# Making one more operand of the first convolution pair inside the preceding program

## The chip, the cores and the metric

The kernel runs on one NeuronCore of a Trainium2 chip. The metric is the device time of one launch in microseconds (us), as the median of several runs.

## The reference

One hybrid encoder block on a sequence of 1024 tokens with 1024 channels, all in float32. A hidden state h is made from x by an RMS norm and a modulation, and is multiplied by one wide weight matrix. Its columns feed two mixers:

```python
proj = h @ w_in
(a_bg, a_cg, a_x, a_z, q, k, v, z_b, a_raw, b_raw, gate_a_raw, gate_b_raw) = split(proj)

ya = a_cg * dwconv_centred(a_bg * a_x, conv_a_w)      # 3 taps
ya = (ya * silu(a_z)) @ w_pa

o  = gated_delta(q, k, v, g, beta), forwards + backwards   # 8 heads, chunks
yb = (rmsnorm(o) * silu(z_b)) @ w_pb

merged = sigmoid(gate_a_raw) * ya + sigmoid(gate_b_raw) * yb
y = rmsnorm(x + gate * (merged @ w_o))
```

The changed lines belong to a_bg, the first of the four products of the convolution mixer.

## The kernel before

**The stages.** After the loads and the first products comes the heads' program, up to about 758 us: eight heads of the delta rule, with the products for k, q, v, z and for the gates ga0 to ga7, gb0 and gb1 filling TensorE in between. Then follow the convolutions (bg, ax, cg, az for pairs of 128-channel blocks, 16 pairs), two pairs of gates (gb2/gb3 and gb4/gb5), two single gates (gb6, gb7), four pairs of the product with w_pa (called pa), then the products with w_pb and w_o.

**Numbers in two parts.** Each float32 operand is split into `hi`, a rounded copy made by ScalarE (ACT), and `lo`, the rest, a subtraction on VectorE (DVE) or GpSimd (POOL). A product is three matmuls: hi by hi, hi by lo, lo by hi.

**Seven products for a pair.** From the convolutions on, a pair of output blocks by two halves of the tokens is computed as a 2 by 2 block product with seven products instead of eight, named A11, A12, A22, S1, S2, S3 and S4 after their weight operand. The weight operands are sums: S1 = A21 + A22, S2 = S1 - A11, S3 = A11 - A21, S4 = A12 - S2. Each product is 4 x 3 matmuls into a bank of PSUM, and products of one bank accumulate on what is there: S3 follows S2 in its bank after S2's value has been copied out (`u2`), A22 follows S3 after `u3` has been read. The token operands (T1 to T4 and parts of h) are made near the end of the heads' program by `early_sums` (L785); for pa they are loaded again (`yop_B`, `yop_T`) and split on ACT and DVE.

**The first pair.** `early_pair` (L825) loads the raw weights of the first bg pair into free buffers of the heads' program, turns them in place into the sums and makes hi and lo of S4 and S2, and, after the mark "begun", of S1 and A22. The products A11 and A12 run at the end of the heads' program. S3 alone is made behind it, by `pairs[0].prep("S3")` and `rest("S3")` (L1491, L1492) from four loads of its own.

**Order.** In the heads' program the instructions of DVE, ACT, POOL and SP (the queue of most DMAs) are ordered by the kernel's own planner, by priority among what is ready: `early_pair` has priority 3, `early_sums` 4, a smaller number goes first. From the convolutions on, these engines run in the order in which the program is written. In the loop over `steps` (product by product), `advance` makes the weights of the product five steps ahead: `prep` the sums and hi, `rest` lo.

**Buffers.** `xpads` (L459) are three padded rows, used in turn in the heads' program and, two of them, by the convolutions; their four outer columns are zero. The weights of the seven products get their buffers from `slots` (L1288), by a counter that runs through six places and is carried on from pair to pair, into pa:

```python
    place, spare = [4], []
    def slots(name):
        i, place[0] = place[0], (place[0] + 1) % 6
        if i > 3:
            return [btile(p, f"w{p}{name}", 2, dtype=F32R) for p in "hl"]
        if i % 2 == 0 or not spare:
            spare[:] = [wp.tile([P, KT * P], F32R, tag=f"w{p}", name=f"w{p}{name}") for p in ("hi", "lo")]
        return [t[:, ch(i % 2, 512)] for t in spare]
```

The tags `whi` and `wlo` have two buffers each. The same tags serve `wtile` (L1254), which makes whole weights for the single gates gb6 and gb7 four steps before the end of the loop (L1567), and for the products with w_pb. A tile's buffer is free for the next tile of its tag when every instruction of the program that reads or writes the tile, wherever it is written, has run.

**The tail of the loop.** After the last steps (A22, A11, A12, S4 of the pair gb4) the program has, in this order: the splits of the `yop_B` tiles (8), gate 6 (`gate_block(6)`, L1577), four more splits of `yop_B` and four of `yop_T`, the weights of pa's first five products (A11, A12, S4, S2, S1, L1582), gate 7 (L1584), twelve loads of `yop_T`, and the loop over pa's products, which splits two of these tiles a step (T1, then T3, then T4).

Of the kernel before, what the change touches and what calls it, by code (L numbers as in the profile page):

```python
# [9 lines left out]
F32 = mybir.dt.float32  # L10
F32R = mybir.dt.float32r
AF = mybir.ActivationFunctionType
ALU = mybir.AluOpType
# [3 lines left out]
P = 128  # L17
T = 1024
# [310 lines left out]
def block(ctx: ExitStack, tc: tile.TileContext, x, c, wada, wadag, badaT, nwT, win, wab, cva, cvq,  # L329
          alog, dtb, gnw, wpa, wpb, wo, fnw, out, dbg=None):  # L330
    nc = tc.nc
    sched = Scheduler(nc.tensor)
    V, S, G, Q = (Engine(sched, n, e) for n, e in (("dve", nc.vector), ("act", nc.scalar), ("pool", nc.gpsimd),
                                                   ("dma", nc.sync)))
# [33 lines left out]
    def ch(c, w=P):  # L368
        return slice(w * c, w * c + w)
# [13 lines left out]
    def tile_of(pl, shape, tag, name, bufs, dtype=F32):  # L383
        return "tile", pl, shape, tag, name, bufs, dtype
# [11 lines left out]
    weights, wanted, early = {}, [], {}  # L396
# [38 lines left out]
    gc_ = ctx.enter_context(tc.tile_pool(name="gc", bufs=1))  # L435
# [20 lines left out]
    G.affine_select(out=maskB, in_=maskB, pattern=[[-1, P]], compare_op=ALU.is_ge, fill=NEG,  # L456
                    base=0, channel_multiplier=1)
    masks = (maskF, maskB)
    xpads = [gc_.tile([P, T + 4], F32, name=f"xpad{i}") for i in range(2)]  # L459
    for xp in xpads:  # L460
        G.memset(xp[:, 0:2], 0.0)
        G.memset(xp[:, T + 2 : T + 4], 0.0)
# [8 lines left out]
    def rows_of(name, h):  # L471
        return tile_of(gq, [P, T], f"{name}T", f"{name}T{h}", {"k": 3, "q": 2}[name])
# [279 lines left out]
    def big(tag, name, bufs=1, dtype=F32):  # L752
        return tile_of(gp if bufs < 3 else tp, [P, T], tag, name, bufs, dtype)
# [71 lines left out]
    def early_pair():  # L825

        yield "need", ("out", H - 2)
        yield "need", ("pq", H - 1)
        yield "need", ("z", H - 1)
        yield "need", ("w", "bg0")  # L830
        raw = []
        for b, (tag, src) in enumerate((("qT", win[A_BG + 1]), ("tmp", win[A_BG]))):
            t = yield (rows_of("q", H) if tag == "qT" else big(tag, f"first{b}", 2))
            Q.dma_start(t, src)
            raw += [t[:, 0:512], t[:, 512:T]]
        a21, a22, a11, a12 = raw
        V.tensor_tensor(a21, a21, a22, ALU.add)
        V.tensor_tensor(a11, a21, a11, ALU.subtract)
        V.tensor_tensor(a12, a12, a11, ALU.subtract)
        for mark, names, raws in (("filled", ("S4", "S2"), (a12, a11)), ("begun", ("S1", "A22"), (a21, a22))):  # L840
            yield "need", mark
            hi = yield tile_of(wp, [P, KT * P], "whi", f"wh_{names[0]}", 2, F32R)
            lo = yield tile_of(wp, [P, KT * P], "wlo", f"wl_{names[0]}", 2, F32R)
            for i, (n, t) in enumerate(zip(names, raws)):
                h, l = early[n] = [w[:, ch(i, 512)] for w in (hi, lo)]
                S.activation(h, t, AF.Copy)
                V.tensor_tensor(l, t, h.bitcast(F32), ALU.subtract)

    npad = [2]

# [340 lines left out]
    def fill():  # L1191
# [41 lines left out]
        for half, n in enumerate(("A11", "A12")):  # L1233
            ps = early[n] = yield get(pp, f"ps_first_{n}", weights["bg0"][0])
            for m in range(4):
# [3 lines left out]

    sched.run([(chain(h), 0) for h in range(H)] + [(merge(h), 0) for h in range(H)] + [head_out(h) for h in range(H)]  # L1240
              + [g for h in range(H) for g in ((prep_k(h), 1), prep_q(h))] + [fill(), loader(2), (early_pair(), 3), (early_sums(), 4)])
    gctx.close()
    V, S, G, Q, PE = nc.vector, nc.scalar, nc.gpsimd, nc.sync, nc.tensor
# [34 lines left out]
    def btile(tag, name, bufs, shape=(P, 512), dtype=F32):  # L1278
        return late_pools[tag].tile(list(shape), dtype, tag=tag, name=name, bufs=bufs)
# [120 lines left out]
    def mixed(name, j0, place):  # L1400
        seen = [0, 0]

        def full(n, b):
            if (n, b) not in outs:
                outs[n, b] = btile("out", f"{n}{j0 + b}", 4, (P, T))
            return outs[n, b]

        def consume(b, half, ps, add):
            sl = ch(half, 512)
            x = xpads[b][:, 2 + 512 * half : 514 + 512 * half]  # L1410
            seen[b] += 1
            if name in ("bg", "cg"):
                dst = x if name == "bg" else full("c", b)[:, sl]
                if add is None:
                    S.activation(dst, ps, AF.Copy)
                else:
                    V.tensor_tensor(dst, ps, add, ALU.add)
                return
            t = ps
            if add is not None or name == "az":  # L1420
                t = btile("tmp", f"t_{name}{j0}{b}{half}", 2)
                if add is not None:
                    V.tensor_tensor(t, ps, add, ALU.add)
                    ps = t
                if name == "az":
                    S.activation(t, ps, AF.Silu)
            if name == "ax":
                V.tensor_tensor(x, t, x, ALU.mult)
                if seen[b] == 2:
                    acc = full("a", b)  # L1430
                    late.extend(partial(conv3, acc, b, j0 + b, i) for i in range(3))
                return
            c, a = outs["c", b], outs["a", b]
            V.tensor_tensor(t, t, c[:, sl], ALU.mult)
            V.tensor_tensor(a[:, sl], t, a[:, sl], ALU.mult)
            if seen[b] == 2:
                Q.dma_start(y_d[j0 + b], a)
            if sum(seen) == 4:
                rows = [outs.pop((n, b)) for n in ("a", "c") for b in range(2)]
                late.extend([None] * (4 if j0 < 6 else 0) + [partial(y_sum, j0 // 2, i, *rows) for i in range(4)])  # L1440

        return Pair(name, j0, consume, place)

    def y_sum(m, i, a0, a1, c0, c1):
# [31 lines left out]
    pairs = [(n, j) for j in range(0, 8, 2) for n in ("bg", "ax", "cg", "az")]  # L1476
    pairs = [mixed(n, j, None if i else "first") for i, (n, j) in enumerate(pairs)]
# [9 lines left out]
            S.activation(xp[:, 2 + 512 * half : 514 + 512 * half], ps, AF.Sigmoid)  # L1487
        Q.dma_start(sgb_d[j], xp[:, 2 : T + 2])

    pairs[0].ops.update({n: early[n] for n in ("S4", "S2", "S1", "A22")})  # L1490
    pairs[0].prep("S3")  # L1491
    pairs[0].rest("S3")  # L1492
    for n in ("A11", "A12"):
        steps.pop(0)
        pairs[0].after(n, early[n])
# [282 lines left out]
def build(nc, arrays, dbg=None, **kw):  # L1778
    aps = {n: nc.dram_tensor(f"in_{n}", a.shape, mybir.dt.from_np(a.dtype), kind="ExternalInput").ap()
           for n, a in arrays.items()}  # L1780
    out = nc.dram_tensor("out_0_dram", (1, 1024, 1024), F32, kind="ExternalOutput").ap()
    with tile.TileContext(nc, **kw) as tc:
        block(tc, *aps.values(), out, **({"dbg": dbg} if dbg else {}))
# [11 lines left out]
```

## Time and profile before

| what | value |
| --- | --- |
| time, median of 3 runs | 1402.9 us (1399.78 to 1403.99) |
| time of the profiled execution | 1401.2 us |
| its span, first to last instruction | 1399.5 us |
| mean granted TensorE clock | 0.994 |
| PE busy from 778 to 1000 us | 222.00 of 222.00 us |
| PE busy from 1000 to 1160 us | 155.66 of 160.00 us |

The span is what the profile's positions count from; the execution's own time is 1.7 us more. PE is TensorE; matmuls overlap in the pipeline, so a busy PE is not a PE at its peak, but a pause of PE is time lost wherever PE sets the end.

### The profile page before, as it was taken

The numbers are of one execution on the slowest core, as the hardware profiler recorded it, in microseconds if no ns is written. First come the engines' busy times: TensorE is split into PE (matmuls) and PEld (weight loads), VectorE is DVE, ScalarE is ACT, GpSimd is POOL, SyncE is SP. The second block draws the span as 40 slices with busy tenths as digits, with TensorE's granted clock in tenths as the row PEclk, the third lists the DMA queues.
The fourth block names the chain that finished last, engine by engine and source line by source line (L and its number), as shares of the span: only waits on it lengthen the run. The fifth ranks groups of instructions, "written<-read, shape, count | busy, mean of one in ns | idle before, by whom it ended". The sixth has DMA issues, their size and how long they took to land.

```text
span 1399.5 us, 22490 instructions
## 1 busy us (share of the span) xinstructions
PE 1357.9 (97%) x8450; PEld 1132.6 (81%) x8450; DVE 918.7 (66%) x1591; ACT 633.0 (45%) x1543; POOL 461.9 (33%) x702
## 2 busy tenths in 40 slices
PE   5899999999999999999999999999999999999998
PEld 5678888897888888888888788888887878778886
DVE  6868175666758675858585777777787487663335
ACT  5447675564747475654535232232323453323211
POOL 2004847573647565665511000000000100276401
PEclk9999999999999999999999999999999999999999
DMA  9325332505033231414123113131311585595502
GB/s 358 100 56 159 113 80 80 152 32 151 31 88 95 81 102 42 133 41 104 50 103 135 61 54 112 46 120 61 118 49 76 196 300 181 189 333 177 188 15 106
DMA packets 129489, 163.33 MB, mean 117 GB/s; under 512 B 75234, under 2 KB 75618, under 8 KB 129379
## 3 DMA queue, kind: packets, MB, share of 16 engines
q1 hardware_dynamic: 128946, 160.58, 35.5%
q8 instruction: 66, 1.08, 0.3%
q10 hardware_dynamic: 432, 1.31, 0.3%
q14 instruction: 45, 0.36, 0.1%
HBM read 128.16 MB, written 33.69 MB: 116 GB/s over the span
## 4 chain that ended last, share of the span: by engine, by line
PE 88%; DVE 5%; DMA 2%; issue 2%; ACT 1%; POOL 1%; SPq 1%; POOLq 0%; DVEq 0%; ACTq 0%
PE pp_ga L215 6%; PE pp_z L215 6%; PE cb L215 6%; PE pp_q L215 5%; PE pp_v L215 5%; PE pp_k L215 5%; PE ps_cg_S L1353 4%; PE o L215 4%; PE ps_ax_S L1353 4%; PE ps_az_S L1353 4%; PE ps_bg_S L1353 3%; PE ps_pa_S L1353 3%; PE fo L1699 2%; PE fo L1700 2%; PE fo L1701 2%
## 5 line engine op out<-in xcount | busy, mean ns | idle before, releaser
L323 POOL TENSOR_TENSOR E<-E,et 128x30 f32<-128x30 f32 (+7 forms) x240 | 117.5, 490 | 16.9
L1260 POOL TENSOR_TENSOR wl_gb<-wr_gb,wh_gb 128x512 fp32r<-128x512 f32 x4 | 5.6, 1411 | 348.5 <-ACT wh_gb L1259 345.6
L323 POOL TENSOR_TENSOR et<-E 128x30 f32<-128x30 f32 (+7 forms) x240 | 110.2, 459 | 30.8 <-DMA E<-s 14.1
L323 DVE SCALAR_TENSOR_TENSOR S<-S,exps,cb 128x128 f32<-128x128 f32 x96 | 29.7, 344 | 59.7 <-PE cb L215 59.0
L323 ACT ACTIVATE vw<-cb,cols 128x128 f32<-128x128 f32 x112 | 36.1, 363 | 68.8 <-PE cb L215 68.5
L1260 POOL TENSOR_TENSOR wl_pb<-wr_pb,wh_pb 128x512 fp32r<-128x512 f32 x16 | 23.5, 1471 | 119.8 <-ACT wh_pb L1259 119.7
L215 PE MATMUL pp_z<-hhi,wh_z 128*128 128x512 f32 x128 | 52.8, 412 | 0.0
L215 PE MATMUL pp_z<-hhi,wl_z 128*128 128x512 f32 x128 | 52.7, 412 | 0.0
L215 PE MATMUL pp_z<-hlo,wh_z 128*128 128x512 f32 x128 | 52.7, 412 | 0.0
L1270 PE MATMUL pp_pb<-bhi,wl_pb 128*128 128x512 f32 x128 | 50.9, 398 | 1.7 <-POOL wl_pb L1260 1.7
L1269 PE MATMUL pp_pb<-blo,wh_pb 128*128 128x512 f32 x128 | 50.6, 395 | 1.8 <-DVE blo L1550 1.8
L215 PE MATMUL pp_ga<-hhi,wl_ga 128*128 128x512 f32 x128 | 51.7, 404 | 0.0
L215 PE MATMUL pp_ga<-hhi,wh_ga 128*128 128x512 f32 x128 | 51.6, 403 | 0.0
L215 PE MATMUL pp_ga<-hlo,wh_ga 128*128 128x512 f32 x128 | 51.5, 402 | 0.0
L323 DVE SCALAR_TENSOR_TENSOR r<-cb,negeg,vp 128x128 f32<-128x128 f32 x112 | 34.3, 344 | 25.8 <-PE cb L215 25.5
L1268 PE MATMUL pp_pb<-bhi,wh_pb 128*128 128x512 f32 x128 | 51.1, 399 | 0.0
L323 ACT ACT_TABLE_LOAD x38 | 48.8, 1283 | 1.4 <-PEq L1790 0.8
L323 DVE SCALAR_TENSOR_TENSOR vT<-xpad,cvq_t,vT 128x1024 f32<-128x1024 f32 x32 | 48.7, 1522 | 0.3
L215 PE MATMUL pp_q<-hhi,wl_q 128*128 128x512 f32 x112 | 44.9, 401 | 2.2 <-issue 2.2
L323 ACT ACTIVATE vn<-cb,cols 128x128 f32<-128x128 f32 x128 | 41.3, 371 | 10.4 <-PE cb L215 10.4
L323 DVE SCALAR_TENSOR_TENSOR qT<-xpad,cvq_t,qT 128x1024 f32<-128x1024 f32 x32 | 45.7, 1427 | 0.3
L215 PE MATMUL pp_q<-hhi,wh_q 128*128 128x512 f32 x112 | 45.8, 409 | 0.0
(951 smaller groups left out, 4419.7 us busy)
## 6 DMA issues: line engine op xcount, KB each, us to landing
wada<-in_wada SPq DMA_DIRECT2D x16, 512.0 KB, 8.4
D<-gr_d SPq DMA_DIRECT2D x16, 512.0 KB, 6.7
wr_bg<-in_win SPq DMA_DIRECT2D x18, 256.0 KB, 2.7
xt<-in_x SPq DMA_DIRECT2D x8, 512.0 KB, 8.5
wr_k<-in_win SPq DMA_DIRECT2D x16, 256.0 KB, 2.6
wr_q<-in_win SPq DMA_DIRECT2D x16, 256.0 KB, 2.6
wr_v<-in_win SPq DMA_DIRECT2D x16, 256.0 KB, 3.1
wr_ga<-in_win SPq DMA_DIRECT2D x16, 256.0 KB, 2.7
```

What stands on the lines that cost most here:

```text
L215: getattr(self.pe, what)(out, *ins, **kw)
L323: self._sched.record(self._name, lambda: real(*args, **kw), outs, ins, cost, extra, table, op == "memset", port)
L1260: G.tensor_tensor(lo[:, ch(q, 512)], raw, hi[:, ch(q, 512)].bitcast(F32), ALU.subtract)
L1268: PE.matmul(ps, wh, mhi[k][:, sl], start=i == 0, stop=False)
L1269: PE.matmul(ps, wh, mlo[k][:, sl], start=False, stop=False)
L1270: PE.matmul(ps, wl, mhi[k][:, sl], start=False, stop=i == KT - 1)
L1353: PE.matmul(ps, w, r, start=first and m == i == 0, stop=m == 3 and i == 2, skip_group_check=True)
L1699: PE.matmul(ps, mhi[k][:, ch(t)], wh, start=k == 0, stop=False)
L1700: PE.matmul(ps, mlo[k][:, ch(t)], wh, start=False, stop=False)
L1701: PE.matmul(ps, mhi[k][:, ch(t)], wl, start=False, stop=k == KT - 1)
```

## The change

S3 of the first pair joins the four operands that `early_pair` makes. After "begun", and after S1 and A22, it subtracts A11's place (which holds S2) from A22, which gives S3, into the place of A12, and splits it into the two halves of `xpad1`. The loads, the sum and the split behind the heads' program go away, and with them one call of `slots`. `xpad1` becomes a tile that is given up and taken again: the first `consume` that writes to it takes it anew and sets its outer columns to zero.

```diff
-    xpads = [gc_.tile([P, T + 4], F32, name=f"xpad{i}") for i in range(2)]
+    xpads = [sched.place(gc_.tile([P, T + 4], F32, tag=f"xpad{i}", name=f"xpad{i}", bufs=1), gc_, f"xpad{i}", 1) for i in range(2)]
@@ early_pair
                 S.activation(h, t, AF.Copy)
                 V.tensor_tensor(l, t, h.bitcast(F32), ALU.subtract)
+        t = yield tile_of(gc_, [P, T + 4], "xpad1", "first_S3", 1, F32R)
+        h, l = early["S3"] = [t[:, ch(i, 512)] for i in range(2)]
+        V.tensor_tensor(a12, a22, a11, ALU.subtract)
+        S.activation(h, a12, AF.Copy)
+        V.tensor_tensor(l, a12, h.bitcast(F32), ALU.subtract)
+        xpads[1] = None
@@ mixed, consume
             sl = ch(half, 512)
+            if not xpads[b]:
+                xpads[b] = gc_.tile([P, T + 4], F32, tag=f"xpad{b}", name=f"xpad{b}_again", bufs=1)
+                for i in (0, T + 2):
+                    G.memset(xpads[b][:, i : i + 2], 0.0)
@@ behind the heads' program
-    pairs[0].ops.update({n: early[n] for n in ("S4", "S2", "S1", "A22")})
-    pairs[0].prep("S3")
-    pairs[0].rest("S3")
+    pairs[0].ops.update({n: early[n] for n in ("S4", "S2", "S1", "S3", "A22")})
```

## The prediction

> **What bounds the kernel now.** I read the busy totals and the chain of work that ended last first, then the stretch in which the changed weights are used, then who waited for whom on PE.
>
> ```profile
> PE 1357.9 (97%) x8450; PEld 1132.6 (81%) x8450; DVE 918.7 (66%) x1591; ACT 633.0 (45%) x1543; POOL 461.9 (33%) x702
> ...
> PE 88%; DVE 5%; DMA 2%; issue 2%; ACT 1%; POOL 1%; SPq 1%; POOLq 0%; DVEq 0%; ACTq 0%
> ```
>
> TensorE is busy for 97% and is 88% of the chain. An edit on another engine counts only where PE stands still for it, or where it makes PE stand still. So I look for PE's pauses around the edit.
>
> ```profile
> 758.00:778.00 20.00, 17.90 (x76) 13.50 (x77) 16.35 (x26) 8.16 (x15) 0.00 (x0) 1.00 0.53 185
> ```
> ```profile
> PE ps_bg_S L1353 <- ACT u_bg L1359: 1.0, 1, 1.0
> PE ps_ax_S L1353 <- ACT whS_ax L1331: 0.7, 1, 0.7
> PE ps_bg_S L1353 <- DVE u_bg L1361: 0.4, 1, 0.4
> ```
>
> The first row is 758 to 778 us by engine (PE, PEld, DVE, ACT, POOL): PE lacks 20.00 - 17.90 = 2.1 us, and the three waits are those 2.1 us. That is all the change can win at its own place, 0.15% of the run. DVE is the busiest engine behind PE there (16.35 of 20), POOL does nothing.
>
> **Part one: S3 made early.** Removed: four loads, one DVE subtraction, one ACT copy, one DVE rest. Added in the heads' program: again one subtraction, one copy, one rest, and later two small POOL memsets.
>
> ```profile
> 714.67 0.33 SPq L323 DMA_DIRECT2D sga_d<-xpad  x1
> ...
> 754.24 2.25 SPq L1324 DMA_DIRECT2D wr_bg<-in_win  x4
> ```
> ```profile
> 761.10 0.69 DVE L323 TENSOR_TENSOR sums_ktok<-kT,sums_ktok 128x512 fp32r<-128x512 f32 x1
> ...
> 764.29 1.29 DVE L323 TENSOR_TENSOR sums_ktok<-kT,sums_ktok 128x512 fp32r<-128x512 f32 x2
> 765.50 0.69 DVE L1315 TENSOR_TENSOR S_bg<-wr_bg,wr_bg 128x512 f32<-128x512 f32 x1
> 766.89 0.69 DVE L1338 TENSOR_TENSOR wlS_bg<-S_bg,whS_bg 128x512 fp32r<-128x512 f32 x1 [0.70 <-ACT whS_bg L1331]
> 767.50 0.68 DVE L1417 TENSOR_TENSOR xpad<-ps_first_A,e_bg 128x512 f32<-128x512 f32 x1
> ```
> ```profile
> 767.24 0.59 ACT L1359 ACTIVATE u_bg<-ps_bg_S 128x512 f32<-128x512 f32 x1
> ```
> ```profile
> 763.30 0.62 PE L1353 MATMUL ps_bg_S<-sums_ktok,wh_S 128*128 128x512 f32 x2
> ```
>
> The loads cost nothing: S_bg follows the last sums without a bracket, so it waited for its turn on DVE, not for data. What S3 costs today is 767.50 - 765.50 = 2.0 us of DVE: two operations at 0.6 and the 0.70 in which DVE waits for ACT between them. Moved, the operations come ahead of the late sums (priority 3 against 4) and take 2 x 0.6 = 1.2 us there, with no gap because other sums fill it. Gain 2.0 - 1.2 = **0.8 us** for xpad, for u_bg on ACT and so for PE's start on S3; the two later pauses move along. What they push back is covered: sums_ktok, the last one that product S2 needs, ends at 761.8 today and is wanted from 763.30 by PE, 1.5 us of slack for 1.2. Should that cover fail, it costs up to 1.2 us; should the two find idle DVE time, the gain reaches 2.1. The memsets wait for product S3 on an idle POOL, and their columns are read only by the first convolution: nothing. The added wait, for xpad1 to be free, is over by then: of the 32 uses of the three buffers in turn the third-last falls to xpad1, the last ga gate, whose store left SP at 714.67, 40 us earlier. On SP the later loads move up by four, to no use.
>
> **Part two: the shifted places.** The call that goes away also moved a counter. `slots` is called 18 x 7 - 2 - 4 = 120 times in the convolutions and gates before (A11, A12 and the four early operands never call it), 119 times after; call c, from 0, gets place (4 + c) mod 6. Places 4 and 5 have buffers of their own (names wh, wl); 0 and 1, and 2 and 3, are the halves of one tile `whi`/`wlo`, which has two buffers. In between this costs nothing: between 778 and 1000 no wait on PE is listed, and pairs already occur with all six places. At the end it matters. Before, the last call gets place 3, the tile is full. After, the last (S4 of gate pair 4) gets place 2, and the **next call, A11 of the first pa pair, gets place 3: the second half of that same old tile**, though both `wtile` calls for gates 6 and 7 come between. A tile's buffer is handed on after the last instruction of the program that touches it, so this one is kept until product A11 of pa. Gate 6 takes the other buffer; gate 7 has none until gate 6's products are through.
>
> ```profile
> 1100.76 1.15 ACT L1259 ACTIVATE wh_gb<-wr_gb 128x512 fp32r<-128x512 f32 x2 [7.54 <-PE ps_gb_A L1353]
> 1106.20 1.33 ACT L1259 ACTIVATE wh_gb<-wr_gb 128x512 fp32r<-128x512 f32 x2 [4.29 <-PE ps_gb_S L1353]
> 1107.44 0.58 ACT L1359 ACTIVATE e_gb<-ps_gb_A 128x512 f32<-128x512 f32 x1
> ```
> ```profile
> 1103.48 0.39 PE L1353 MATMUL ps_gb_S<-hhi,whiA_gb 128*128 128x512 f32 x1
> ...
> 1106.23 0.39 PE L1268 MATMUL pp_gb<-hhi,wh_gb 128*128 128x512 f32 x1
> ...
> 1117.22 0.39 PE L1268 MATMUL pp_gb<-hhi,wh_gb 128*128 128x512 f32 x1
> ```
>
> The first two rows show exactly these hand-overs: gate 6's copies wait for A11 (the last of its buffer's two), gate 7's for S4. After, gate 6 waits for A12 (PE begins S4 at 1103.48), still ahead of its product at 1106.23; gate 7's copies wait for the end of gate 6's products, the last matmul before 1117.22, about 1117.4 with its length, instead of 1106.20. Queued behind them on ACT is all of the tail in program order, e_gb first: 1117.4 + 1.15 = 1118.55 against 1107.44, **11.1 us later**.
>
> ```profile
> 1122.64 1.14 ACT L1331 ACTIVATE whA_pa<-wr_pa 128x512 fp32r<-128x512 f32 x2
> 1126.73 1.15 ACT L1331 ACTIVATE whiS_pa<-S_pa 128x512 fp32r<-128x512 f32 x2 [2.95 <-DVE S_pa L1315]
> 1128.23 0.63 ACT L1331 ACTIVATE whiS_pa<-S_pa 128x512 fp32r<-128x512 f32 x1 [0.35 <-PE pp_gb L1269]
> 1128.77 1.07 ACT L1487 ACTIVATE xpad<-pp_gb 128x512 f32<-128x512 f32 x2
> ...
> 1134.60 1.32 ACT L1549 ACTIVATE yop_T<-yop_T 128x512 fp32r<-128x512 f32 x2 [2.23 <-DMA yop_T<-t_d]
> ```
> ```profile
> 1123.89 0.69 DVE L1338 TENSOR_TENSOR wlA_pa<-wr_pa,whA_pa 128x512 fp32r<-128x512 f32 x1
> ...
> 1135.27 1.38 DVE L1550 TENSOR_TENSOR yop_T<-yop_T 128x512 fp32r<-128x512 f32 x2 [3.44 <-ACT yop_T L1549]
> ```
> ```profile
> 1129.87 0.33 SPq L1488 DMA_DIRECT2D sgb_d<-xpad  x1
> 1130.28 7.02 SPq L1546 DMA_DIRECT2D yop_T<-t_d  x12
> ```
> ```profile
> 1128.67 0.39 PE L1353 MATMUL ps_pa_A<-yop_B,wlA_pa 128*128 128x512 f32 x1
> ```
>
> PE first: gate 7's products start some 2 us late (copy, then the bank that e_gb frees). Then pa's A11 wants wlA_pa, today done at 1124.6 and used at 1128.67; 11.1 later it is done at 1135.7, so PE stands **7.0 us** later there. The chain behind is later still. The S1 copy that waits for gate 7's products today has no such wait then and follows its two neighbours: 1126.73 + 11.1 + 1.04 = 1138.87 (two copies in a run; the second adds 1.15 - 0.63 = 0.52), the sigmoids at 1139.4 against 1128.77, 10.65 later. Behind them stands, in SP's order, the store sgb_d, and behind that the twelve loads of yop_T, so the split of T1 begins 10.65 later on ACT and DVE, at 1145.9 on DVE. PE, 7.0 later, reaches T1's third part before it and waits.
>
> ```profile
> 1143.69 0.69 DVE L1550 TENSOR_TENSOR yop_T<-yop_T 128x512 fp32r<-128x512 f32 x1
> ...
> 1152.07 1.28 DVE L1550 TENSOR_TENSOR yop_T<-yop_T 128x512 fp32r<-128x512 f32 x2
> ```
> ```profile
> 1144.43 0.50 PE L1353 MATMUL ps_pa_S<-yop_T,whiS_pa 128*128 128x512 f32 x1 [0.62 <-DVE yop_T L1550]
> ...
> 1150.24 0.70 PE L1353 MATMUL ps_pa_S<-yop_T,whA_pa 128*128 128x512 f32 x2 [1.59 <-ACT yop_T L1549]
> ...
> 1152.81 0.50 PE L1353 MATMUL ps_pa_S<-yop_T,whA_pa 128*128 128x512 f32 x1 [0.71 <-DVE yop_T L1550]
> ```
>
> Today DVE already sets the pace here: from 1135.27 on it works through its list nearly without a gap, and PE waits for it at 1144.43, 1150.24 and 1152.81. The list doesn't change, so its end, and PE's at 1152.81, moves by about **10.6 us**. Bounds of this part: if DVE and ACT caught up wholly, PE would keep its 7.0 and lose today's 0.62 + 1.59 + 0.71 = 2.9 us of pauses, so 4.1; at most it is the full 11.1. I take 10.6, as those three waits show DVE binding.
>
> **Sum.** +10.6 - 0.8 = +9.8 us. On the profiled execution, 1401.2 us with a span of 1399.5, that is 1411.0; on the median of the three runs, 1402.9, it is **1412.7 us**, the number I give.
>
> **Rivals.** *The old tile is not kept* (not slower): gate 7's copies start at 1106.20 as now because the buffer goes on regardless of the later use of its second half. The place is the hand-over at L1567; price of the tail 0; it decides if gate 7's copies still wait for S4. Then only part one is left: 1402.9 - 0.8 = 1402.1, at best 1400.8. Against it: today's rows wait for the last user of each tile, and overwriting gate 7's weights before their product would spoil the result. *The chain catches up*: ACT has slack behind the splits and DVE loses its gaps; tail 4.1 to 7.0, so 1406 to 1409. For it: ACT is busy for only 45% of the run; against: DVE's list has hardly a gap. *The clock falls*: PE would pause over 4 us ahead of A11 and again in S1 to A22.
>
> ```profile
> 47.43 0.67 PE L215 MATMUL k<-hlo,wh_k 128*128 128x512 f32 x1 [1.95 <-DVE hlo L323]
> ```
> ```profile
> 48.00:49.00 1.00, 1.00 (x4) 0.81 (x3) 1.00 (x3) 0.84 (x2) 0.00 (x0) 0.50 0.58 174
> ```
>
> After such a pause the granted clock was 0.50 and four matmuls started in 1 us, about half as many as at full clock. Ahead of A11 a drop hides, since PE then waits for DVE anyway, 10.6 - 7.0 = 3.6 us; only one at A22 counts. Gate 6's 48 matmuls take 1117.22 - 1106.23 = 11.0, so a product of 12 takes 2.75 and at half clock up to 2.75 more; for a part of it I estimate 1.6: 1414.3. Against it: today's three pauses by A22 left the clock alone. [...]
>
> **Chances.** The forecast (tail 7 to 11.1) 0.66; clock 0.11; catching up 0.08; tile not kept 0.15. The range takes in the first three: from full catching up with part one at its best, 1402.9 + 4.1 - 2.1 = 1405, to 1402.9 + 11.1 + 1.6 + 1.2 = 1416.8, rounded to 1416.5. About 0.3% (4.2 us) can be told from no change: faster 0.01; same 0.17 (tile not kept, and 0.03 of catching up); slower 0.82.
>
> **What would show it.** In the changed kernel: the first S3 product starts 0.8 us earlier against S1's end; gate 7's copies on ACT begin after gate 6's products, with PE pp_gb as releaser; PE pauses of some 2 us inside the gates and 4 us ahead of pa's A11; the twelve yop_T loads leave SP 10 to 11 us later. If wh_gb still waits for ps_gb_S, part two is wrong; if A11 is 7 later but A22's end is not 10 later, the pace of DVE is.

## The result, and the profile after

| | before | changed |
| --- | --- | --- |
| median of 6 runs each | 1402.36 us (1399.78 to 1404.09) | 1409.88 us (1408.69 to 1412.99) |
| profiled execution | 1401.2 us | 1410.02 us |
| its span | 1399.5 us | 1408.3 us |

The ratio is 1.0057, with a 95% interval of 1.0043 to 1.007: 6.0 to 9.8 us slower. The forecast was 1412.7 us, slower, in a range of 1405 to 1416.5. The measured time is 2.8 us below it and inside the range, and the forecast difference of 9.8 us lies at the upper end of the interval.

First the busy totals and the chain that ended last, of the changed kernel.

```profile
PE 1358.5 (96%) x8450; PEld 1132.5 (80%) x8450; DVE 921.5 (65%) x1591; ACT 631.5 (45%) x1543; POOL 461.8 (33%) x704
...
PE 86%; DVE 6%; DMA 3%; ACT 2%; issue 1%; POOL 1%; SPq 0%; POOLq 0%; DVEq 0%; ACTq 0%
```

TensorE does the same 8450 matmuls in nearly the same busy time (1358.5 us, 1357.9 before). The chain went through DVE, DMA and ACT for more of the run: DVE 5% to 6%, DMA 2% to 3%, ACT 1% to 2%. So what grew was not TensorE's work but its waiting. Who waited is in the list of PE's waits from 700 us on (total, times, longest):

```profile
PE ps_pa_A L1359 <- ACT whiS_gb L1337: 4.0, 1, 4.0
PE ps_pa_S L1359 <- DVE yop_T L1558: 2.8, 3, 1.5
PE pp_pb L1276 <- POOL wl_pb L1266: 2.7, 2, 2.5
PE pp_pb L1275 <- DVE blo L1558: 1.8, 1, 1.8
PE ps_pa_S L1359 <- ACT yop_T L1557: 1.6, 1, 1.6
PE pp_gb L1274 <- ACT e_gb L1365: 1.5, 1, 1.5
PE ps_gb_S L1359 <- DVE u_gb L1367: 1.3, 1, 1.3
PE ps_ax_S L1359 <- ACT whS_ax L1337: 0.7, 1, 0.7
PE ps_bg_S L1359 <- DVE u_bg L1367: 0.4, 1, 0.4
```

The last two are what is left of the three waits around S3 that the prediction quoted; the one of 1.0 for `u_bg` on ACT is gone. That is part one. The first row is new, and its name tells the story of part two: pa's first product waits for weights in a tile called `whiS_gb`. The name is the one under which the tile was made, for S4 of the last gate pair; A11 of pa was written into its second half.

**Part one.** DVE's timeline: S3 is subtracted and its rest made ahead of the late sums. The two DVE rows between them, left out here, are the rest of another early operand and a row of the heads' output. `xpad` follows later.

```profile
757.41 0.68 DVE L323 TENSOR_TENSOR first<-qT,first 128x512 f32<-128x512 f32 x1
...
759.27 0.68 DVE L323 TENSOR_TENSOR first_S<-first,first_S 128x512 fp32r<-128x512 f32 x1
...
766.14 0.68 DVE L1427 TENSOR_TENSOR xpad<-ps_first_A,e_bg 128x512 f32<-128x512 f32 x1
```

To measure the gain across two executions one needs a mark in each. I take the last store `sga_d` in SP's queue, quoted in the prediction at 714.67 for the kernel before, and PE's start on S3 of the last gate pair, some 360 us later and ahead of the tail. The stage between them holds part one and, by the prediction, nothing of part two; that is nearly so.

SP's queue of the changed kernel:

```profile
714.32 0.33 SPq L323 DMA_DIRECT2D sga_d<-xpad  x1
```

PE's timeline of the kernel before:

```profile
1075.75 0.73 PE L1353 MATMUL ps_gb_S<-sums_D,whS_gb 128*128 128x512 f32 x2 [1.42 <-DVE u_gb L1361]
```

PE's timeline of the changed kernel (the second row is used below):

```profile
1074.19 0.73 PE L1359 MATMUL ps_gb_S<-sums_D,whS_gb 128*128 128x512 f32 x2 [1.28 <-DVE u_gb L1367]
...
1134.03 0.80 PE L1359 MATMUL ps_pa_A<-yop_B,wloS_gb 128*128 128x512 f32 x1 [0.16 <-DVE wloS_gb L1344]
```

From mark to mark: 1075.75 - 714.67 = 361.08 before, 1074.19 - 714.32 = 359.87 after, so 1.2 us were won in this stage. Not all of it is S3's move. The runs e1 and e2 below separate the two halves of the change: with the same places, S3's move is worth 361.08 - 360.08 = 1.00 us and 360.88 - 359.87 = 1.01 us, and the shifted places alone 361.08 - 360.88 = 0.20 us. The 1.0 is the wait for `u_bg` that is gone.

**Part two.** ACT's timeline of the changed kernel, from the gates' weights on:

```profile
1101.92 1.15 ACT L1265 ACTIVATE wh_gb<-wr_gb 128x512 fp32r<-128x512 f32 x2 [9.94 <-PE ps_gb_A L1359]
...
1115.70 1.15 ACT L1265 ACTIVATE wh_gb<-wr_gb 128x512 fp32r<-128x512 f32 x2 [12.63 <-PE pp_gb L1275]
1116.76 0.58 ACT L1365 ACTIVATE e_gb<-ps_gb_A 128x512 f32<-128x512 f32 x1
...
1131.98 0.62 ACT L1337 ACTIVATE whiS_gb<-wr_pa 128x512 fp32r<-128x512 f32 x1
...
1137.64 1.07 ACT L1497 ACTIVATE xpad_again<-pp_gb 128x512 f32<-128x512 f32 x2
...
1143.39 1.31 ACT L1557 ACTIVATE yop_T<-yop_T 128x512 fp32r<-128x512 f32 x2 [2.16 <-DMA yop_T<-t_d]
```

Gate 7's copies stood idle for 12.63 us and were released by `pp_gb`, gate 6's products, where S4 (`ps_gb_S`) released them before. Everything behind them is late: `e_gb`, A11 of pa, the sigmoids, and by way of SP's queue the loads of `yop_T`:

```profile
1138.73 0.33 SPq L1498 DMA_DIRECT2D sgb_d<-xpad_again  x1
1139.15 7.72 SPq L1554 DMA_DIRECT2D yop_T<-t_d  x12
```

and with them DVE's list of splits, T1 first and T4 last:

```profile
1144.05 1.37 DVE L1558 TENSOR_TENSOR yop_T<-yop_T 128x512 fp32r<-128x512 f32 x2 [2.89 <-ACT yop_T L1557]
...
1160.58 1.29 DVE L1558 TENSOR_TENSOR yop_T<-yop_T 128x512 fp32r<-128x512 f32 x2
```

The last of these splits was at 1152.07 before. From the mark at S3 of the gates it took 1152.07 - 1075.75 = 76.32 us before and 1160.58 - 1074.19 = 86.39 after: **the tail is 10.07 us longer**. I use this distance, S3 of the gates to the last split of T4, as the measure of the tail in every run below. The whole difference of the two spans is then 8.8 = -0.35 (the heads' program, up to the first mark) - 1.21 (the stage between the marks: part one, and 0.2 of the shift) + 10.07 (the tail) + 0.29 (what follows the tail).

### The profile page after: what moved, and what is told of

Its sections match the earlier page's. It is cut to its first block, busy times and chain, and to the rows that moved or that the text cites. A ratio compares the mean times of both kernels' runs of the same rounds, so it can differ in the third digit from the quotient of the medians.

```text
span 1408.3 us, 22489 instructions
## 1 busy us (share of the span) xinstructions
PE 1358.5 (96%) x8450; PEld 1132.5 (80%) x8450; DVE 921.5 (65%) x1591; ACT 631.5 (45%) x1543; POOL 461.8 (33%) x704
## 4 chain that ended last, share of the span: by engine, by line
PE 86%; DVE 6%; DMA 3%; ACT 2%; issue 1%; POOL 1%; SPq 0%; POOLq 0%; DVEq 0%; ACTq 0%
PE pp_ga L215 6%; PE pp_z L215 6%; PE pp_q L215 6%; PE cb L215 6%; PE pp_v L215 6%; PE pp_k L215 5%; PE ps_cg_S L1359 4%; PE o L215 4%; PE ps_ax_S L1359 4%; PE ps_az_S L1359 4%; PE ps_bg_S L1359 3%; PE ps_pa_S L1359 2%; PE fo L1707 2%; PE fo L1708 2%; PE fo L1709 2%; PE ps_gb_S L1359 2%
## 5 line engine op out<-in xcount | busy, mean ns | idle before, releaser
L323 POOL TENSOR_TENSOR et<-E 128x30 f32<-128x30 f32 (+7 forms) x240 | 116.0, 483 | 29.7 <-DMA E<-s 13.0
L323 POOL TENSOR_TENSOR E<-E,et 128x30 f32<-128x30 f32 (+7 forms) x240 | 115.0, 479 | 16.8
L323 ACT ACTIVATE vn<-cb,cols 128x128 f32<-128x128 f32 x128 | 41.3, 372 | 10.4 <-PE cb L215 10.4
L215 PE MATMUL pp_q<-hlo,wh_q 128*128 128x512 f32 x112 | 45.8, 409 | 0.0
```

The source lines that it names most:

```text
L215: getattr(self.pe, what)(out, *ins, **kw)
L323: self._sched.record(self._name, lambda: real(*args, **kw), outs, ins, cost, extra, table, op == "memset", port)
```

## The experiments

The theory: the lost call of `slots` leaves the last tile of the gates half full; pa fills its other half; so the tile is held and gate 7 has no buffer. The main rival for each step stands with the run. Each ratio is taken against the kernel before as it ran beside the kernel in question: a median of 1402.36 us for the changed kernel, 1401.54 for e1 to e4, 1401.60 for e5 to e8.

| run | median | ratio to before (95%) | tail against before |
| --- | --- | --- | --- |
| changed kernel | 1409.88 | 1.0057 (1.0043 to 1.007) | +10.07 |
| e1: changed, counter starts at 5 | 1400.34 | 0.999 (0.9981 to 0.9999) | +0.08 |
| e2: before, counter starts at 3 | 1411.24 | 1.0066 (1.0048 to 1.0083) | +10.07 |
| e4: changed, counter starts at 2 | 1408.51 | 1.0048 (1.0032 to 1.0064) | +10.09 |
| e3: changed, half-full tile dropped | 1405.05 | 1.0025 (1.0008 to 1.0042) | +4.72 |
| e8: e3, gate 7's raw weights in other buffers | 1401.40 | 1.0 (0.9988 to 1.0013) | +0.24 |
| e5: changed, gate 7's weights made later | 1408.44 | 1.0048 (1.0029 to 1.0067) | +7.95 |
| e6: changed, gate 7's store behind the loads | 1409.83 | 1.0055 (1.0034 to 1.0075) | +8.03 |
| e7: e1 and e6 together | 1400.01 | 0.9987 (0.9975 to 0.9998) | +0.02 |

**e1: the counter put right, part one kept.**

```diff
-    place, spare = [4], []
+    place, spare = [5], []
```

> The changed kernel with the counter of places started at 5 in place of 4, so that every operand after S3 gets the place it had before the change. Theory (the tail is lost through the half-filled tile that gate 7 cannot have): gate 7's copies wait for product S4 again, the splits of T1 and T4 begin where they did in the kernel before or about 1.2 us earlier, and the time is that of before less part one, 1402.4 - 1.2 = 1401.2 us. Rival (making S3 early, with the loads that move up, costs the time): about 1410 us, as the changed kernel.

It gave 1400.34 us, 0.999 of before, so it beats both kernels, if by a hair. PE's timeline and DVE's, SP's queue, and ACT's timeline of e1:

```profile
1071.56 0.73 PE L1359 MATMUL ps_gb_S<-sums_D,whS_gb 128*128 128x512 f32 x2 [1.42 <-DVE u_gb L1367]
```
```profile
1147.96 1.29 DVE L1558 TENSOR_TENSOR yop_T<-yop_T 128x512 fp32r<-128x512 f32 x2
```
```profile
711.48 0.33 SPq L323 DMA_DIRECT2D sga_d<-xpad  x1
```
```profile
1102.08 1.31 ACT L1265 ACTIVATE wh_gb<-wr_gb 128x512 fp32r<-128x512 f32 x2 [4.29 <-PE ps_gb_S L1359]
```

Gate 7's copies wait for S4 again, with the 4.29 us of the kernel before, and the tail is back to 76.40. Between the two marks lie 360.08 us, 1.0 less than before. So the whole loss hangs on the counter, and part one by itself is a gain.

**e2: the kernel before, with the counter moved and nothing else.**

```diff
-    place, spare = [4], []
+    place, spare = [3], []
```

> The kernel before with the counter started at 3 in place of 4, so that the places of all operands after S3 are those of the changed kernel; S3 is made and loaded as before. Theory: gate 7's copies wait for gate 6's products, PE pauses 1.5 us in the gates and 4 us ahead of pa's A11, and the tail loses the 10.1 us that the changed kernel's loses between the gate pairs and the last split of T4: 1402.4 + 10.1 = 1412.5 us. Rival (making S3 early costs the time): 1402.4 us, as before.

It is slower, at 1.0066, with none of S3's move in it. PE's waits, PE's timeline, DVE's timeline and SP's queue of e2:

```profile
PE ps_pa_A L1353 <- ACT whiS_gb L1331: 4.0, 1, 4.0
...
PE pp_gb L1268 <- ACT e_gb L1359: 1.5, 1, 1.5
```
```profile
1078.48 0.73 PE L1353 MATMUL ps_gb_S<-sums_D,whS_gb 128*128 128x512 f32 x2 [1.28 <-DVE u_gb L1361]
```
```profile
1164.87 1.29 DVE L1550 TENSOR_TENSOR yop_T<-yop_T 128x512 fp32r<-128x512 f32 x2
```
```profile
717.60 0.33 SPq L323 DMA_DIRECT2D sga_d<-xpad  x1
```

The same two pauses, to the tenth of a microsecond, and the same tail: 1164.87 - 1078.48 = 86.39. From mark to mark it took 360.88 us, close to before (361.08), since S3 stands at its old place; the 0.2 are the shift's. With e1 this takes the change apart: the counter alone loses, S3's move alone wins.

**e4: another start that leaves the tile half full.** The last call of `slots` gets place 2 in the changed kernel. Starting at 2 it gets place 0, and A11 of pa place 1, so another tile is half full at the same point.

```diff
-    place, spare = [4], []
+    place, spare = [2], []
```

> The changed kernel with the counter started at 2: the last operand of the gate pairs then gets place 0, and pa's A11 place 1, again the second half of an old tile, though all the other places differ from the changed kernel's. Theory: gate 7's copies wait for gate 6's products and the time is about 1410 us as in the changed kernel (within 2 us). Rival (the order of places as such): no reason to be slow, 1401 to 1404 us like the start at 5.

1.0048, and a tail of +10.09. PE's waits of e4:

```profile
PE ps_pa_A L1359 <- ACT whiS_gb L1337: 4.0, 1, 4.0
```

So it isn't a matter of one special buffer but of the half at which the count stops.

**e3: drop the half-full tile by hand.** With `spare` emptied behind the two `wtile` calls, A11 of pa starts a new tile, and the old one ends with S4.

```diff
             ws = [wtile(win[G_B + j], f"gb{j}") for j in (6, 7)]
+            spare.clear()
```

> The changed kernel, places as in it, but the half-filled tile is forgotten once the weights of gates 6 and 7 have been asked for, so that pa's A11 takes a new tile. Theory: gate 7's copies wait for S4 again and the 10 us are gone; S2 of pa, a tile of its own, now waits for gate 7's products on ACT, one operand earlier than in the kernel before, which may cost up to 1 us: 1401 to 1402.5 us. Rival (it is the other order of places, which operand waits for which product, that costs): about 1410 us, since the places are unchanged.

This expectation failed: 1405.05 us, 3.5 us over the 1401.54 us of the kernel before beside it. The pause ahead of A11 was gone, so the held tile was indeed dropped, but gate 7's copies were late for another reason. ACT's timeline of e3:

```profile
1107.56 0.63 ACT L1265 ACTIVATE wh_gb<-wr_gb 128x512 fp32r<-128x512 f32 x1 [3.99 <-DMA wr_gb<-in_win]
1109.52 0.63 ACT L1265 ACTIVATE wh_gb<-wr_gb 128x512 fp32r<-128x512 f32 x1 [1.33 <-DMA wr_gb<-in_win]
```

They wait for their raw weights. These are loaded into the same two buffers as gate 6's and so only after gate 6's copies, which in this kernel wait for A12 instead of A11 (the shift moved gate 6's buffer too). That is a second, smaller chain in the shifted kernel, which the long wait for the held tile covers. Counted from the mark at S3 of the gates, `e_gb` came 3.7 us later than in the kernel before, against 4.72 for the whole tail. The remaining 1.0 us isn't assigned; a lower clock may have a part in it (mean granted clock of the profiled execution 0.992, against 0.994 before), but no window here shows where it was lower inside this tail.

**e8: e3, and gate 7's raw weights in other buffers**, two of the eight that the pairs' raw weights use in turn.

```diff
-            ws = [wtile(win[G_B + j], f"gb{j}") for j in (6, 7)]
+            raws6 = wraws(win[G_B + 6], "gb6")
+            raws7 = [btile("raw", f"wr_gb7_{q}", 8) for q in range(2)]
+            for q, raw in enumerate(raws7):
+                Q.dma_start(raw, win[G_B + 7][:, ch(q, 512)])
+            ws = [wtile(None, f"gb{j}", r) for j, r in ((6, raws6), (7, raws7))]
+            spare.clear()
```

> The kernel with the half-filled tile forgotten, with gate 7's raw weights in two buffers of their own, so that their loads no longer wait for gate 6's copies and rests. Theory for the 3.5 us that were left there: gate 6's buffer is given up one product later (A12 instead of A11), which moved gate 7's loads and with them all of ACT's tail by 3.7 us; with own buffers gate 7's copies start when S4 is through, and the time is 1401 to 1402 us. Rival (the order of places inside pa costs them): 1405 us.

The ratio is 1.0, the tail +0.24: what e3 had left was due to those loads. ACT's timeline of e8 has gate 7's copies wait for S4 again:

```profile
1105.90 1.15 ACT L1265 ACTIVATE wh_gb<-wr_gb 128x512 fp32r<-128x512 f32 x2 [1.59 <-PE ps_gb_S L1359]
```

**e5: let the queue behind gate 7's copies go first.** Raw loads where they were, the copies written behind gate 6's block, the tile still held.

```diff
-            ws = [wtile(win[G_B + j], f"gb{j}") for j in (6, 7)]
+            ws = [wtile(win[G_B + j], f"gb{j}") for j in (6,)]
+            raws7 = wraws(win[G_B + 7], "gb7")
...
     gate_block(6, ws[0])
+    ws.append(wtile(None, "gb7", raws7))
```

> The changed kernel, gate 7's weights still without a buffer until gate 6's products are through, but their copies written behind gate 6 in the program (its raw weights are loaded where they were), so that ACT does the rest of the gate pairs and eight splits before it comes to the wait. Theory (what costs 10 us is what stands on ACT behind the waiting copies): e_gb comes at about 1103 us instead of 1116.8; PE now waits for gate 7's weights themselves, about 4 to 4.5 us, and the end moves by that, less part one: 1404.5 us. Rival (gate 7's late weights cost the 10 us whatever stands behind them): 1410 us.

1408.44 lies between the theory's number and the rival's. The ratio's interval, 1405.7 to 1411.0 us, shuts out the theory's 1404.5 and not the rival's 1410; the tail, at 7.95, has neither some 4 nor the whole 10.07. ACT's queue did run early, but PE then paused for gate 7's weights themselves. PE's waits of e5, then ACT's timeline, SP's queue and the windows around the pause:

```profile
PE pp_gb L1274 <- ACT wh_gb L1265: 4.6, 1, 4.6
```
```profile
1119.32 1.15 ACT L1265 ACTIVATE wh_gb<-wr_gb 128x512 fp32r<-128x512 f32 x2
...
1133.73 1.16 ACT L1337 ACTIVATE whiS_pa<-S_pa 128x512 fp32r<-128x512 f32 x2 [3.24 <-PE pp_gb L1275]
```
```profile
1136.30 3.84 SPq L1554 DMA_DIRECT2D yop_T<-t_d  x7
```
```profile
1118.50:1125.00 6.50, 4.86 (x11) 3.36 (x12) 4.67 (x7) 6.50 (x13) 2.98 (x2) 0.50 1.04 402
```

The copies now stand behind gate 6's splits and sigmoids on ACT. PE resumes at 1120.0 with the clock at 0.50 until 1125; half of these 5 us, 2.5 us, is my estimate of what that puts on top of the 4.6. Gate 7's products end late, the copies for S2 and S1 (the `whiS_pa` row) wait for them, and the loads of `yop_T` leave SP at 1136.30 instead of 1130.28: 6.0 later, 8.0 counted from the mark at S3 of the gates, which came 2.0 earlier in this execution. The tail moved by 7.95. So gate 7's products, when they are late themselves, move the loads just as ACT's queue does. The run supports the step from the loads to the end of the tail, and shows that this reordering of ACT brings back only 2.1 of the 10.07 us.

**e6: the store of gate 7 behind the twelve loads**, so that on SP the loads no longer wait for the sigmoids.

```diff
-    gate_block(7, ws[1])
+    gate_block(7, ws[1], False)
...
             fetch_operand(n, m, hp.tile([P, T], F32R, tag=f"h{p}{k}", name=f"yop_{n}_{m}", bufs=1))
+    Q.dma_start(sgb_d[7], xpads[1][:, 2 : T + 2])
```

> The changed kernel with gate 7's store to sgb_d written behind the twelve loads of yop_T in SP's order, so that these loads no longer wait for gate 7's sigmoids on ACT. Theory (T1's loads behind the store are late, and the splits that follow them set the pace of pa's first pair): the loads leave SP at about 1130 us, when gate 7's products are through, instead of 1139.15; ACT reaches the splits of T1 2.2 us earlier, as it waited 2.16 us for the loads, and the end comes about 2 us earlier: 1407.9 us. Rival (the 7 us at A11 are what counts, the loads only follow): within 0.5 us of 1409.9 us.

By time the rival's number came out: 1409.83 against 1409.88. SP's queue and the windows of e6:

```profile
1132.32 8.00 SPq L1555 DMA_DIRECT2D yop_T<-t_d  x12
```
```profile
1258.50:1261.50 3.00, 3.00 (x8) 2.34 (x7) 1.20 (x2) 0.64 (x2) 2.32 (x2) 0.50 0.96 348
```

The loads left 6.8 us earlier than in the changed kernel (8.5 counted from the mark at S3 of the gates, at 1075.86 here), and the tail shortened from 10.07 to 8.03, the 2 us that the theory asked for. But in this execution what follows the tail took 249.9 us against 247.7, and 1.7 of these 2.2 us are, as an estimate, half of a stretch of 3.4 us at a granted clock of 0.50 from 1258 us on (3.0 of it are the row above), which the changed kernel's profiled execution doesn't have. Such a stretch isn't peculiar to the edit: the profiled executions of e1 and e4, without it, also show one behind the tail (0.50 from 1246.5 to 1249 us in e1, means of 0.72 and 0.85 from 1256 to 1260 and to 1264 us in e4), and 249.6 and 249.5 us from the tail to the end. Whether e6 is really worth 2 us is left open: five runs between 1407.8 and 1411.9 us don't show it.

**e7: e1 with the store moved too.**

> The counter started at 5 (nothing of the tail lost) and gate 7's store behind the twelve loads. Theory: the loads leave SP some 1.5 us earlier, ACT's wait for them (2.39 us in the run with the start at 5) shrinks by about that, and of PE's 3.0 us of pauses in pa's first pair 1 to 2 us go: 1400.3 - 1.5 = 1398.8 us. Rival (those pauses come from DVE's list and not from the loads): 1400.3 us.

1400.01, its interval overlapping e1's: no gain that can be told. SP's queue of e7, and its PE timeline:

```profile
1120.67 9.40 SPq L1555 DMA_DIRECT2D yop_T<-t_d  x12
```
```profile
1145.98 0.70 PE L1359 MATMUL ps_pa_S<-yop_T,whA_pa 128*128 128x512 f32 x2 [1.59 <-ACT yop_T L1558]
```

The loads leave 5.5 us earlier than in e1 (1126.16), and yet PE waits its 1.59 us for a `yop_T` split as in the kernel before, and the tail is the same (+0.02). T1's splits did start 2.6 us earlier on ACT (1128.01, against 1130.64 in e1), without a wait for the loads. But the next splits stand on ACT behind a weight copy that came no earlier. ACT's timelines of e1 and e7:

```profile
1135.17 0.63 ACT L1337 ACTIVATE whiA_pa<-wr_pa 128x512 fp32r<-128x512 f32 x1 [1.05 <-PE ps_pa_S L1359]
```
```profile
1135.03 0.63 ACT L1337 ACTIVATE whiA_pa<-wr_pa 128x512 fp32r<-128x512 f32 x1 [3.79 <-issue]
```

In e1 this copy waits for a product of PE; in e7 ACT stands still ahead of it for 3.79 us, with no releaser shown, and starts it at about the same time. With the gates on time, the pauses in pa's first pair seem to come from what stands in order on ACT behind this copy, and not from the loads.

## Why the prediction was right

**The held tile: right.** "Gate 7 has none until gate 6's products are through": the copies' releaser is `pp_gb` (1115.70), e1 and e2 tie it to the counter and to nothing else, and e4 to the half at which the count stops.

**The chain behind it: right, step by step.** From the mark at S3 of the gates, which came 1.56 us earlier than before, the steps moved as follows. `e_gb`: 1116.76 - 1107.44 + 1.56 = 10.9 (forecast 11.1). PE at the first matmul on A11's rest: 1134.03 - 1128.67 + 1.56 = 6.9 (forecast 7.0). Sigmoids: 1137.64 - 1128.77 + 1.56 = 10.4 (10.65). Loads on SP: 1139.15 - 1130.28 + 1.56 = 10.4 (10 to 11). T4's last split: 10.07 (10.6). The two new pauses are 1.5 and 4.0 (some 2, and over 4).

**DVE's pace: right for the changed kernel, a little oversized.** The list "doesn't change", and from T1's split to T4's it took 1160.58 - 1144.05 = 16.5 us against 1152.07 - 1135.27 = 16.8. The 0.3 it caught up, with the sigmoids' 10.4 in place of 10.65, is the 0.5 by which 10.6 was too much. PE's three old pauses are still there (the first grew from 0.62 to 1.54 us), with a fourth of 0.5 ahead of T1's third part, where the prediction had PE arrive before the split. That "those three waits show DVE binding" in the kernel before holds only in part: in e7, which has that kernel's places, T1's splits began 2.6 us earlier, DVE then stood idle for 2.5 us, and the tail did not end earlier. There, as far as the traces show, the copy on ACT set the pace. In the changed kernel DVE's list did follow the loads: in e6, where they left earlier, the tail ended 2.0 us earlier.

**Part one: right in sign, undersized.** 0.8 was forecast, and 1.0 came out between the marks, at the old places (before against e1) as at the shifted ones (e2 against the changed kernel). The 0.2 fit idle time that the prediction left out: in the kernel before, DVE stood idle for about 0.2 us ahead of 757.98 us, and in the changed kernel the row at 757.41 us, S3's subtraction, follows without that gap. In the medians, e1's ratio is a gain of 0.1 to 2.7 us.

**The clock: right that a drop ahead of A11 hides.** The 4 us pause ahead of A11 was followed by 3.4 us of half clock (rows below), and T1's third part still found PE waiting for DVE. With the same pause of 4.0 us e2 had at least 5.0 us of half clock (mean 0.84 from 1133 to 1136 us, 0.50 from 1136 to 1140), and the tail was as long (+10.07), so even that was hidden. The rival "the clock falls" needed a drop at A22; there was none, the granted clock of the changed kernel was 1.00 from 1142 to 1164 us. Two small slips of the prediction change nothing: of the four matmuls counted in the row at 48 us only two started in it (at 48.32 and 48.75 us, against 48 in 11.0 us at full clock), which is what "half as many" needs; and the range's upper end was worked out as 1416.8 and stated as 1416.5.

**What the sum left out.** +10.07 - 1.21 = 8.9 on the profiled execution, where 9.8 was forecast: the tail is 0.5 smaller, and the stage ahead of it won 0.4 more, half of that from the shifted places. The 8.8 measured there fits, but partly by chance: what follows the tail, as long as PE works, holds, as an estimate, 1.7 us lost to half clock before (half of the 3.41 us below) and none after, and 1.0 us more of pauses for `wl_pb` after (2.7 against 1.7), with about 1.0 us that I can't assign. The medians are 7.5 us apart, in an interval of 6.0 to 9.8; where the last microsecond between 7.5 and 8.9 lies isn't settled.

**One step that was priced at nothing and isn't nothing.** "After, gate 6 waits for A12, still ahead of its product" looked only at the product. Gate 6's copies also hold the raw buffers that gate 7's loads need. The longer wait covered it here; uncovered, in e3, the tail was 4.7 us longer, and 0.2 in e8, where the loads had other buffers.

## What to carry to other kernels

A counter or ring that runs on from stage to stage is an output of every stage that uses it: if an edit removes one call, follow the count to the last stage, and ask which buffer is half full where another tag user comes in between. Here starting the count so that it ends even brought the whole 10 us back with one digit (e1). Dropping the half-full tile at the border brought back only 5.4 us of them, until the next stage's raw weights had other buffers too (e3, e8). And when a wait moves, follow not only its result but the buffers that the waiting instruction still holds.

## What the runs showed of the hardware that was not expected

While PE had work, a granted clock of 0.50 came in stretches of 3.41 to 3.42 us in the profiled executions of before (near 34, 48, 338 and 1222 us) and of the changed kernel (near 34, 47, 337 and 1133 us), once after a pause of only 1.80 us, shorter than the 1.95 us at 48 us that the prediction shows. The windows around the one near 1222 us in the kernel before (the third number from the right is the granted clock):

```profile
1221.50:1222.00 0.50, 0.50 (x3) 0.41 (x3) 0.50 (x2) 0.28 (x1) 0.15 (x1) 0.78 0.99 291
1222.00:1225.00 3.00, 3.00 (x8) 2.33 (x8) 0.26 (x1) 0.63 (x1) 2.32 (x2) 0.50 0.74 192
1225.00:1225.50 0.50, 0.50 (x3) 0.36 (x3) 0.00 (x0) 0.00 (x0) 0.35 (x1) 0.81 0.80 123
```

A mean of 0.78 over 0.5 us, between rows of 1.00 and 0.50, means 0.22 us at half clock; with the 3.0 us of the second window and 0.19 us of the third that makes 3.41 us, and, as an estimate, a loss of 1.7 us, half of it. PE's timelines of before and of the changed kernel show the pause ahead of it, and its twin:

```profile
1220.51 0.51 PE L1269 MATMUL pp_pb<-blo,wh_pb 128*128 128x512 f32 x1 [1.80 <-DVE blo L1550]
```
```profile
1228.56 0.50 PE L1275 MATMUL pp_pb<-blo,wh_pb 128*128 128x512 f32 x1 [1.80 <-DVE blo L1558]
```

The same wait of 1.80 us was followed by half clock in one kernel and by full clock in the other. The drop behind the 4 us pause ahead of A11 in the changed kernel has the same length:

```profile
1132.50:1133.00 0.50, 0.35 (x1) 0.35 (x2) 0.50 (x2) 0.50 (x2) 0.00 (x0) 0.68 0.97 344
1133.00:1136.00 3.00, 2.84 (x7) 1.75 (x7) 2.93 (x6) 0.12 (x1) 0.00 (x0) 0.50 0.18 67
1136.00:1136.50 0.50, 0.50 (x4) 0.41 (x3) 0.50 (x2) 0.43 (x1) 0.00 (x0) 0.91 0.00 0
```

0.32 + 3.0 + 0.09 = 3.41 us again. But the same pause didn't always come with the same length: with a 4.0 us pause at the same place, e2 had at least 5.0 us at half clock (from about 1135 us on), and e5, with one of 4.6 us, had 6.8 us (0.71 from 1118.0 to 1118.5 us, 0.50 until 1125.0, 0.96 until 1125.5). What decides whether a pause of 1.80 us is followed by a drop, and how long the drop lasts, no run here shows.
